# A float32 hybrid decoder block on one core: weights' high parts first and low parts after them in each projection, the first two projections interleaved, tokens in eight pieces, and TensorE kept on a constant before the first layer norm

## The chip, the core and the metric

The kernel runs on one core of one Trainium2 chip. The metric is the device time in microseconds (us) of one execution. Beside it stands one profiled execution, whose trace gives the start and length of each engine's instructions: TensorE (PE; its weight loads are PEld), VectorE (DVE), ScalarE (ACT), GpSimd (POOL) and SyncE (SP), which issues most transfers. Columns and ns are as the profile prints them.

## The reference, cut to what matters

One layer, 256 tokens of 2048 features, all in float32:

```python
h = layer_norm(x, emb_ln_g, emb_ln_b)
mix = hybrid_mixer(h, w_in, ...)          # see below
h = layer_norm(ALPHA * h + mix, ln1_g, ln1_b)
ffn = conv_ffn(h, w_ffn_up, ffn_conv_w, ffn_conv_b, w_ffn_down)
h = layer_norm(ALPHA * h + ffn, ln2_g, ln2_b)

def hybrid_mixer(x, w_in, ..., w_out):
    h = x @ w_in                          # 2048 -> a, gate, q, f, i, og, 1024 each
    u = causal_dwconv(a * sigmoid(gate), conv_w, conv_b)      # 31 taps
    u = silu(group_layer_norm(u))                             # 8 groups of 128
    fg = lb + (1 - lb) * sigmoid(f)       # lb: gate bounds, from a softmax over lb_logits
    o = hgrn2_recurrence(silu(q), 1 - fg, i, log(fg))         # 8 heads of 128
    o = rms_norm(o) * hgrn_norm_g * silu(og)
    return concatenate([u, o]) @ w_out

def conv_ffn(x, w_up, conv_w, conv_b, w_down):                # 2 x 5632 features
    g, v = split(x @ w_up)
    return (silu(causal_dwconv(g, conv_w, conv_b)) * v) @ w_down
```

## The kernel before

Every big product is made with float32r operands in three matmuls: an operand is split into a high part (its float32r rounding) and a low part (the rest), and high x high, high x low and low x high are added up in PSUM. Weights come in 196 chunks `raw` of 1 MB (two buffers); ACT copies each half of a chunk to `wh`, DVE subtracts to get `wl` (six buffers each). This is `stream`. The tokens, transposed to features x tokens, stand in `xT`: for each of 16 tiles `k` of 128 features 256 columns of high parts and 256 of low parts.

- A **feature unit** (`mm_features`, used for gate, a, f, q and the FFN's up projection) makes 2 x 128 output features for 256 tokens. For each k and each of its two accumulators it issues one matmul with `wh` over the 512 columns of `xT[k]` and one with `wl` over the 256 high columns: 32 pairs.
- A **token unit** (`mm_tokens`: v, og, the output projection, the down projection) uses tokens as the stationary operand, and issues three matmuls of 512 columns per k and token tile.

`UNITS` gives the mixer's order: ("ag", 0) is gate and a of the first 256 channels, then ("ag", 1), ("v", 0) and so on. Between the halves of a unit `pump()` lets generators advance: the 31 tap operations of a convolution on DVE (L368), its norm `conv_tail` (transposes L377 on PE, statistics L384 and L386 on DVE, the power on POOL L387/L388, L390 on DVE, ACT L392, transposes back L396 on PE), and the recurrences. Four PSUM banks hold accumulators (`acc`), four hold everything else (`ps`).

The start: four transfers of 512 KB bring the tokens `z`; DVE makes the statistics of the two token tiles (L284, L165), POOL the reciprocal root (L166, L167), ACT normalises tile 0 and DVE tile 1 (L179, L181); 32 transposes (L200) in eight groups of two k-tiles; ACT or DVE apply gain and bias (L187, L189), ACT writes the high part and DVE the low part of `xT` (L205). The second layer norm (ln1) lies between the last token units of the mixer and the first FFN unit; there tile 0 is normalised and transposed while PE still works on tile 1.

The tile framework orders each engine's instructions by priority in program order and by a cost model; `tc.issue_after` adds an order without a wait. Each engine executes its instructions in that order. It also gives transfers eight semaphores in turn, so that a ninth is issued only when the first has landed.

Of the kernel before, what the change touches and what calls it, by code (L numbers as in the profile page):

```python
# [34 lines left out]
PAD = 48  # L35
LEVELS = (1, 2, 4, 8, 16, 32, 64)
# [24 lines left out]
def hybrid_block(ctx, tc, x, wts, par, masks, ident_in, emb_g, emb_b, ln1_g, ln1_b, ln2_g, ln2_b, out):  # L61
# [15 lines left out]
    xv = x[0].rearrange("(t p) d -> p t d", p=P)  # L77
    for t in range(2):
# [3 lines left out]
    ident = const.tile([P, P], F32, name="ident")  # L82
    DMA.dma_start(out=ident, in_=ident_in)
# [7 lines left out]
    load_chunk()  # L91
    ps_par = const.tile([P, NPAR], F32, name="ps_par")
    DMA.dma_start(out=ps_par, in_=par)

# [10 lines left out]
    def stream(n):  # L105

        for _ in range(n):
            if nhalf[0] // 2 + 1 < wts.shape[0]:
                load_chunk()
            raw = raws.pop(0)  # L110
            for h in range(2):
# [3 lines left out]
                with ExitStack() as order:  # L115
                    order.enter_context(tc.high_priority(offset=AHEAD if nhalf[0] > 3 else 0))
                    for ins in behind.pop(nhalf[0], ()):
                        order.enter_context(tc.issue_after(ins.ins))
                    S.activation(wh, r, AF.Copy)  # L119
                    V.tensor_tensor(wl, r, wh.bitcast(F32), ALU.subtract)  # L120
# [41 lines left out]
    def layer_norm_stats(st):  # L162
# [3 lines left out]
        G.tensor_scalar(rs, mv[:, 1:2], LN_EPS, None, ALU.add)  # L166
        G.tensor_tensor(rs, rs, mhalf[:, 0:1], ALU.pow)  # L167
        return mv, rs

    def normalise(t, mv, rs, engines):  # L170

        if S in engines:
            nm = small.tile([P, 1], F32, name="nm")
            G.tensor_scalar(nm, mv[:, 0:1], -1.0, None, ALU.mult)
            G.tensor_tensor(nm, nm, rs, ALU.mult)
# [15 lines left out]
    def transpose_split(tiles, nk, gname, bname):  # L191
# [3 lines left out]
        for k0 in range(0, KT, nk):  # L195
# [10 lines left out]
            if tiles[-1] == 1 and (k0 + nk) % 4 == 0:  # L206
                behind[nhalf[0] + (k0 + nk) // 4] = made
# [14 lines left out]
    def mm_features(nch):  # L222


        acc = [accp.tile([P, 2 * T], F32, name="acc") for _ in range(2)]
        k = 0
        for wh, wl in stream(2):
            for kk in range(4):
                for j in range(2):
                    cs = slice(kk * 256 + j * P, kk * 256 + (j + 1) * P)  # L230
# [4 lines left out]
                k += 1  # L235
            pump()
        return acc
# [42 lines left out]
    stats = []  # L280
    for t in range(2):
# [3 lines left out]
        stats.append(layer_norm_stats(st))  # L285
    normalise(0, *stats[0], (S, S, S, S))
    normalise(1, *stats[1], (V, V, V, V))
# [17 lines left out]

    mk = const.tile([P, P + 64 * (len(LEVELS) - 1)], F32, name="mk")
    DMA.dma_start(out=mk, in_=masks)


    lb = const.tile([P, NT], F32, name="lb")  # L310
    omlb = const.tile([P, NT], F32, name="omlb")
    lmax = small.tile([P, NT], F32, name="lmax")
    le = small.tile([P, 2, NT], F32, name="le")
    lsum = small.tile([P, NT], F32, name="lsum")
    V.tensor_tensor(lmax, pc("lg0", 0, NT), pc("lg1", 0, NT), ALU.max)
    V.tensor_tensor(le[:, 0], pc("lg0", 0, NT), lmax, ALU.subtract)
    V.tensor_tensor(le[:, 1], pc("lg1", 0, NT), lmax, ALU.subtract)
# [190 lines left out]
    for kind, i in UNITS:  # L508
        run[kind](i)
# [204 lines left out]
```

## Time and profile before

| | |
|---|---|
| three runs | 1174.7, 1178.58 and 1179.71 us, median 1178.58 |
| the profiled execution | 1176.21 us, of which the span from first to last instruction is 1174.4 us |
| busy | PE 1141.5 us (97%), PEld 978.1, DVE 836.4 (71%), ACT 579.3 (49%), POOL 20.9 |
| chain that ended last | PE 92%, DVE 5% |
| granted TensorE clock | 0.995 over the span |
| transfers | 217.62 MB, mean 185 GB/s; a chunk `raw` of 1 MB lands 4.8 us after its issue (median) |

A busy share is a sum over stages, and PE's includes time that overlaps between matmuls, so what a stage costs is read from the starts of successive instructions. The views used are the waits per engine, the timeline (start, length, instruction, how often, and in brackets the idle time of the engine before it and what ended it), the groups of instructions in a stretch, and the windows (busy time of each engine in a stretch).

### The profile page before, as it was taken

What the parts mean: (1) busy time and instruction counts of PE and PEld (TensorE: products, weight loads), DVE (VectorE), ACT (ScalarE), POOL (GpSimd) and SP (SyncE); (2) the same over time, 40 slices, a digit from 0 to 9 for tenths busy, and PEclk for the clock granted to TensorE, in tenths of its full rate; (3) what the DMA queues carried; (4) which work ended last, traced back from release to release, by engine and by line L of the source; (5) the groups of instructions that cost most, each with busy time, mean ns of one, the idle gap of its engine ahead of it and who ended that gap; (6) DMA issues with size and microseconds to landing.
All of it is one profiled execution on the core that took longest, in us unless ns stands there. A gap on an engine that the chain in (4) does not pass through costs nothing.

```text
span 1174.4 us, 15650 instructions
## 1 busy us (share of the span) xinstructions
PE 1141.5 (97%) x6102; PEld 978.1 (83%) x6102; DVE 836.4 (71%) x1307; ACT 579.3 (49%) x826; POOL 20.9 (2%) x41
## 2 busy tenths in 40 slices
PE   5999999999999989999999999999999999999996
PEld 4887888888888868888888888888888888888885
DVE  7799999998697787666666668444566666665555
ACT  6545655646444355555555553333455554554330
POOL 1000000000000000000000000000000000000001
PEclk9999999999999999999999999999999999999998
DMA  5654544454455536655555557555555555555551
GB/s 217 231 200 179 184 175 148 176 179 144 148 175 188 198 117 246 213 186 184 196 195 180 189 206 233 198 197 184 199 190 181 179 188 193 193 179 183 208 182 72
DMA packets 33050, 217.62 MB, mean 185 GB/s; under 512 B 3664, under 2 KB 3792, under 8 KB 7632
## 3 DMA queue, kind: packets, MB, share of 16 engines
q1 hardware_dynamic: 32112, 214.53, 51.6%
q10 hardware_dynamic: 864, 2.10, 0.5%
q8 instruction: 48, 0.79, 0.3%
q14 instruction: 26, 0.21, 0.1%
HBM read 214.51 MB, written 2.10 MB: 184 GB/s over the span
## 4 chain that ended last, share of the span: by engine, by line
PE 92%; DVE 5%; issue 1%; POOL 1%; DMA 1%; ACT 0%; DVEq 0%; SPq 0%; ACTq 0%
PE acc L231 36%; PE acc L233 19%; PE acc L248 11%; PE acc L250 11%; PE acc L249 11%; PE ps L450 2%; DVE wl L120 1%; DVE y L368 1%; DMA z<-in_x 1%; DVE xT L205 0%; DVE full L189 0%; DVE z L584 0%; DVE z L581 0%; PE ps L200 0%; PE ps L439 0%
## 5 line engine op out<-in xcount | busy, mean ns | idle before, releaser
L231 PE MATMUL acc<-xT,wh 128*128 128x512 f32 x1920 | 674.9, 396 | 0.2
L120 DVE TENSOR_TENSOR wl<-raw,wh 128x1024 fp32r<-128x1024 f32 x392 | 477.8, 1222 | 238.2 <-ACT wh L119 237.8
L119 ACT ACTIVATE wh<-raw 128x1024 fp32r<-128x1024 f32 x392 | 412.1, 1057 | 379.4 <-PE acc L250 203.9
L233 PE MATMUL acc<-xT,wl 128*128 128x256 f32 x1920 | 539.1, 281 | 0.8 <-DVE wl L120 0.8
L231 PEld LDWEIGHTS acc<-xT,wh 128*128 128x128 f32 x1920 | 360.3, 188 | 83.6 <-DVE xT L205 0.7
L233 PEld LDWEIGHTS acc<-xT,wl 128*128 128x128 f32 x1920 | 363.1, 189 | 1.7 <-DVE wl L120 1.5
L249 PE MATMUL acc<-wl,acthi 128*128 128x512 f32 x350 | 136.2, 389 | 0.0
L250 PE MATMUL acc<-wh,actlo 128*128 128x512 f32 x350 | 136.2, 389 | 0.0
L248 PE MATMUL acc<-wh,acthi 128*128 128x512 f32 x350 | 136.2, 389 | 0.0
L368 DVE SCALAR_TENSOR_TENSOR y<-upad,ps_par,y 128x256 f32<-128x256 f32 x240 | 102.6, 476 | 0.0
L241 ACT ACTIVATE tb<-acc 128x256 f32<-128x256 f32 x120 | 44.7, 377 | 81.4 <-PE acc L233 81.4
L250 PEld LDWEIGHTS acc<-wh,actlo 128*128 128x128 f32 x350 | 65.7, 188 | 13.8
L249 PEld LDWEIGHTS acc<-wl,acthi 128*128 128x128 f32 x350 | 65.7, 188 | 13.7
L248 PEld LDWEIGHTS acc<-wh,acthi 128*128 128x128 f32 x350 | 65.7, 188 | 13.5
L248 PE MATMUL acc<-wh,xT 128*128 128x512 f32 x128 | 51.2, 400 | 0.0
L248 PE MATMUL acc<-wh,mixhi 128*128 128x512 f32 x128 | 51.1, 399 | 0.0
L250 PE MATMUL acc<-wh,mixlo 128*128 128x512 f32 x128 | 50.4, 393 | 0.0
L250 PE MATMUL acc<-wh,xT 128*128 128x512 f32 x128 | 50.2, 392 | 0.0
L249 PE MATMUL acc<-wl,mixhi 128*128 128x512 f32 x128 | 50.1, 392 | 0.0
L249 PE MATMUL acc<-wl,xT 128*128 128x512 f32 x128 | 49.9, 390 | 0.0
L567 ACT ACTIVATE acthi<-vv 128x256 fp32r<-128x256 f32 x44 | 18.4, 418 | 53.7 <-DVE vv L566 53.7
L242 DVE TENSOR_TENSOR gpad<-acc,tb 128x256 f32<-128x256 f32 x44 | 18.7, 424 | 25.2 <-ACT tb L241 25.2
(125 smaller groups left out, 711.3 us busy)
## 6 DMA issues: line engine op xcount, KB each, us to landing
raw<-in_wts SPq DMA_DIRECT2D x196, 1024.0 KB, 4.8
z<-in_x ACTq DMA_DIRECT2D x2, 512.0 KB, 5.9
z<-in_x SPq DMA_DIRECT2D x2, 512.0 KB, 5.7
gb<-in_emb_g SPq DMA_DIRECT2D x4, 256.0 KB, 3.4
bb<-in_emb_b SPq DMA_DIRECT2D x4, 256.0 KB, 4.5
gb<-in_ln_g SPq DMA_DIRECT2D x4, 256.0 KB, 4.4
bb<-in_ln_b SPq DMA_DIRECT2D x4, 256.0 KB, 4.7
g<-in_ln_g SPq DMA_DIRECT2D x1, 1024.0 KB, 4.7
```

What stands on the lines that cost most here:

```text
L119: S.activation(wh, r, AF.Copy)
L120: V.tensor_tensor(wl, r, wh.bitcast(F32), ALU.subtract)
L231: PE.matmul(acc[j], lhsT=wh[:, cs], rhs=xT[:, k, :], start=k == 0, stop=False, skip_group_check=True)
L233: PE.matmul(acc[j][:, T:], lhsT=wl[:, cs], rhs=xT[:, k, 0:T], start=False, stop=k == KT - 1, skip_group_check=True)
L241: S.activation(tb, acc[:, T:], AF.Copy)
L242: V.tensor_tensor(dst, acc[:, 0:T], tb, ALU.add)
L248: PE.matmul(acc, lhsT=hi(k + i), rhs=wh[:, cs], start=k + i == 0, stop=False)
L249: PE.matmul(acc, lhsT=hi(k + i), rhs=wl[:, cs], start=False, stop=False)
L250: PE.matmul(acc, lhsT=lo(k + i), rhs=wh[:, cs], start=False, stop=k + i == nk - 1)
L368: V.scalar_tensor_tensor(y[i], ups[i][:, k:k + T], pc("conv_w", c * TAPS + k), y[i], ALU.mult, ALU.add)
L450: PE.matmul(sp[0:m, 2 * i + s], lhsT=K[:, i, s * P:s * P + m], rhs=rhs, start=True, stop=True)
L567: S.activation(acthi[:, slot], vv, AF.Copy)
```

## The change

- **Feature units run in two passes** (`high`, `low`): all 32 matmuls with `wh`, then all 32 with `wl`. `pump` stays at four calls per unit.
- **The first unit ("ag", 0) interleaves gate and a** (`mm_features_by_k(2)`): for each half chunk the gate's high and low matmuls, then those of a; the weights are laid out so that chunks come in that order. Four accumulators are in use.
- **The first FFN unit goes by token tile** (`mm_features_by_tile`): the high matmuls of tile 0 over all k (2 x 128 columns each), then those of tile 1 with the low ones.
- Tokens load in eight pieces of 256 KB, alternating between the SP and ACT queues; the identity after the first four, parameters before the first `raw`.
- 28 matmuls over a zeroed part of `xT` are issued to PE ahead of everything (`WARM`).
- The gate bounds (`masks_and_bounds`, seven small DVE operations, one on ACT, one transfer) follow the first unit.
- In ln1, tile 0 is normalised on ACT, tile 1 in turns on DVE and ACT; the product of minus the mean is one DVE operation (`minus_mean`).

```diff
+WARM = 28
...
-        for c in range(2):
-            eng = DMA if c == 0 else S
-            eng.dma_start(out=z[:, t, c * 1024:(c + 1) * 1024], in_=xv[:, t, c * 1024:(c + 1) * 1024])
...
+        for c in range(4):
+            eng = (DMA, S)[c % 2]
+            eng.dma_start(out=z[:, t, c * 512:(c + 1) * 512], in_=xv[:, t, c * 512:(c + 1) * 512])
+        if t == 0:
+            DMA.dma_start(out=ident, in_=ident_in)
...
+    idle = xT[:, KT - 1, :]
+    V.memset(idle.bitcast(F32), 0.0)
+    blank = psp.tile([P, 512], F32, name="ps")
+    for n in range(WARM):
+        PE.matmul(blank, lhsT=idle[:, 0:P], rhs=idle, start=True, stop=True)
...
-            if tiles[-1] == 1 and (k0 + nk) % 4 == 0:
-                behind[nhalf[0] + (k0 + nk) // 4] = made
+            mark[0] = made
+            n = (k0 + nk) // 4
+            if (k0 + nk) % 4 == 0 and len(tiles) == 2:
+                behind[nhalf[0] + 2 * n, "high"] = behind[nhalf[0] + 2 * n + 1, "high"] = made
...
-    def mm_features(nch):
...
-                    PE.matmul(acc[j], lhsT=wh[:, cs], rhs=xT[:, k, :], start=k == 0, stop=False,
-                              skip_group_check=True)
-                    PE.matmul(acc[j][:, T:], lhsT=wl[:, cs], rhs=xT[:, k, 0:T], start=False,
-                              stop=k == KT - 1, skip_group_check=True)
...
+    def high(acc, wh, n):
+
+        for kk in range(4):
+            for j in range(2):
+                PE.matmul(acc[j], lhsT=wh[:, kk * 256 + j * P:kk * 256 + (j + 1) * P], rhs=xT[:, 4 * n + kk, :],
+                          start=n + kk == 0, stop=False, skip_group_check=True)
+
+    def low(acc, wl, n):
+
+        for kk in range(4):
+            for j in range(2):
+                PE.matmul(acc[j][:, T:], lhsT=wl[:, kk * 256 + j * P:kk * 256 + (j + 1) * P],
+                          rhs=xT[:, 4 * n + kk, 0:T], start=False, stop=4 * n + kk == KT - 1,
+                          skip_group_check=True)
...
+        acc, lows = new_acc(), []
+        for n, (wh, wl) in enumerate(stream(2)):
+            high(acc, wh, n)
+            lows.append(wl)
+            if n in (1, 2):
+                pump()
+        for n, wl in enumerate(lows):
+            low(acc, wl, n)
+            if n in (0, 3):
+                pump()
+        return acc
+
+    def mm_features_by_k(count):
+
+
+        accs = [new_acc() for _ in range(count)]
+        for n, (wh, wl) in enumerate(stream(2 * count)):
+            high(accs[n % count], wh, n // count)
+            low(accs[n % count], wl, n // count)
+        return accs
+
+    def mm_features_by_tile():
...
+        for t in range(2):
+            for n, (wh, wl) in enumerate(parts):
+                for kk in range(4):
+                    for j in range(2):
+                        PE.matmul(tile_of(acc[j], t), lhsT=wh[:, kk * 256 + j * P:kk * 256 + (j + 1) * P],
+                                  rhs=tile_of(xT[:, 4 * n + kk, :], t), start=t + n + kk == 0, stop=False,
+                                  skip_group_check=True)
+                if t == 1:
+                    low(acc, wl, n)
         return acc
...
-        acc = mm_features(2)
+        acc, acc_a = mm_features_by_k(2) if p == 0 else (mm_features(), None)
...
-        acc = mm_features(2)
+        acc = acc_a or mm_features()
...
-                        normalise(t, *layer_norm_stats(st1[t]), (V, V, V, V))
+                        mv, rs = layer_norm_stats(st1[t])
+                        normalise(t, mv, rs, minus_mean(mv, rs, V)[0], (V, S, V, S) if t else (S, S, S, S))
...
-        acc = mm_features(2)
+        acc = mm_features() if j else mm_features_by_tile()
```

How the instructions stand on PE at the start of the program (`ps` are transposes, `acc` matmuls of the first unit; widths are the columns streamed), before:

```order
L200 MATMUL ps<-ident,z 128x128 x24
L231 MATMUL acc<-xT,wh 128x512 x2
L200 MATMUL ps<-ident,z 128x128 x8
L233 MATMUL acc<-xT,wl 128x256 x2
L231 MATMUL acc<-xT,wh 128x512
L233 MATMUL acc<-xT,wl 128x256
```

and of the changed program (L172 is the constant, L219 the transposes, L251 `high`, L258 `low`):

```order
L172 MATMUL ps<-xT 128x512 x28
L219 MATMUL ps<-ident,z 128x128 x24
L251 MATMUL acc<-xT,wh 128x512 x5
L219 MATMUL ps<-ident,z 128x128 x4
L251 MATMUL acc<-xT,wh 128x512 x3
L258 MATMUL acc<-xT,wl 128x256 x4
L219 MATMUL ps<-ident,z 128x128 x4
L258 MATMUL acc<-xT,wl 128x256 x4
```

The constant stands ahead of all transposes; eight high matmuls and then eight low ones replace the pairs, and the last two groups of transposes lie inside the first eight of each.

The second convolution's norm on DVE (`cst` and `cmv` are its statistics, `cnm` minus the mean times the root that POOL makes of `cmv`, `wl` the low part of a later weight, `y` taps of the next convolution), before:

```order
L384 BN_STATS cst<-ps 128x6 x4
L386 BN_AGGR cmv<-cst 128x2 x4
L120 TENSOR_TENSOR wl<-raw,wh 128x1024
L390 SCALAR_TENSOR_TENSOR cnm<-cmv,crs 128x4
L368 SCALAR_TENSOR_TENSOR y_1440<-upad_215,ps_par,y_1440 128x256
```

and of the changed program:

```order
L436 BN_STATS cst<-ps 128x6 x4
L438 BN_AGGR cmv<-cst 128x2 x3
L125 TENSOR_TENSOR wl<-raw,wh 128x1024
L438 BN_AGGR cmv<-cst 128x2
L420 SCALAR_TENSOR_TENSOR y_1522<-upad_251,ps_par,y_1522 128x256
L442 SCALAR_TENSOR_TENSOR cnm<-cmv,crs 128x4
```

A `wl` now stands ahead of the fourth aggregate, for which POOL waits, and a tap ahead of `cnm`.

PE behind the last token matmul of the mixer, where ln1's second token tile is transposed (`ps<-ident,z`) and the first FFN unit begins, before:

```order
L250 MATMUL acc<-wh,mixlo 128x512
L200 MATMUL ps<-ident,z 128x128 x10
L231 MATMUL acc<-xT,wh 128x512
L233 MATMUL acc<-xT,wl 128x256
L231 MATMUL acc<-xT,wh 128x512
L200 MATMUL ps<-ident,z 128x128 x2
```

and of the changed program (L301 are the high matmuls by token tile):

```order
L319 MATMUL acc<-wh,mixlo 128x512
L301 MATMUL acc<-xT,wh 128x2x128 x24
L219 MATMUL ps<-ident,z 128x128 x12
L301 MATMUL acc<-xT,wh 128x2x128 x13
L219 MATMUL ps<-ident,z 128x128 x2
L301 MATMUL acc<-xT,wh 128x2x128 x3
```

24 matmuls that need only token tile 0 now stand ahead of the transposes of tile 1; the other eight of tile 0 stand behind twelve of them.

## Rows read from the trace of the kernel before

**Rows 1.** Waits of PE, whole run: us in total, times, longest us.

```profile
PE ps L200 <- ACT z L179: 11.1, 1, 11.1
PE ps L200 <- DVE z L181: 5.6, 3, 4.0
PE ps L396 <- ACT tmp L392: 3.4, 2, 2.8
PE acc L233 <- DVE wl L120: 0.8, 2, 0.5
```

**Rows 2.** Timeline of PE: pairs, then a token unit, then the last 256-column matmuls.

```profile
619.62 0.39 PE L231 MATMUL acc<-xT,wh 128*128 128x512 f32 x1
...
622.74 0.39 PE L231 MATMUL acc<-xT,wh 128*128 128x512 f32 x1
...
699.82 0.39 PE L250 MATMUL acc<-wh,actlo 128*128 128x512 f32 x1
...
703.90 0.39 PE L250 MATMUL acc<-wh,actlo 128*128 128x512 f32 x1
...
1162.15 0.28 PE L613 MATMUL ps<-wh,acthi 128*128 128x256 f32 x1
...
1163.47 0.28 PE L615 MATMUL ps<-wh,actlo 128*128 128x256 f32 x1
```

**Rows 3.** Timeline of the start, engines mixed; the last row begins pair 65.

```profile
5.41 3.21 DVE L284 BATCH_NORM_STATS2 st<-z 128x6 f32<-128x512 f32 x5 [5.41 <-DMA z<-in_x]
8.54 0.25 DVE L165 BATCH_NORM_AGGREGATE mv<-st 128x2 f32<-128x24 f32 x1
...
10.23 2.93 ACT L179 ACTIVATE z<-z,nm,rs 128x512 f32<-128x512 f32 x4 [2.77 <-POOL nm L175]
...
11.83 1.92 DVE L181 TENSOR_SCALAR z<-z,mv,rs 128x512 f32<-128x512 f32 x4 [1.01 <-POOL rs L167]
...
16.89 0.50 PE L231 MATMUL acc<-xT,wh 128*128 128x512 f32 x1
...
42.27 0.39 PE L231 MATMUL acc<-xT,wh 128*128 128x512 f32 x1
```

**Rows 4.** The page's transfers: issues, KB each, median us from issue to landing.

```profile
out<-z SPq DMA_DIRECT2D x4, 256.0 KB, 2.4
```

**Rows 5.** Groups of ACT and DVE between 11 and 31 us: busy us, mean ns.

```profile
L119 ACT ACTIVATE wh<-raw 128x1024 fp32r<-128x1024 f32 x6 | 6.2, 1051 | 0.0
...
L120 DVE TENSOR_TENSOR wl<-raw,wh 128x1024 fp32r<-128x1024 f32 x6 | 7.1, 1217 | 0.0
L205 DVE TENSOR_TENSOR xT<-full,xT 128x512 fp32r<-128x512 f32 x8 | 5.2, 684 | 1.2 <-ACT xT L205 1.2
L189 DVE TENSOR_SCALAR full<-ps,ps_par 128x256 f32<-128x256 f32 x8 | 4.1, 538 | 0.2
```

**Rows 6.** Timeline of PE: transposes of the start, early and late.

```profile
12.70 2.98 PE L200 MATMUL ps<-ident,z 128*128 128x128 f32 x13
...
16.11 0.71 PE L200 MATMUL ps<-ident,z 128*128 128x128 f32 x5
```

**Rows 7.** Window behind ln1: us, PE busy, granted clock, DMA share, GB/s.

```profile
428.89:432.29 3.40, 3.40 (x12) 0.50 0.33 137
```

**Rows 8.** Timeline of the first convolution's norm: transposes, statistics, transposes back.

```profile
106.03 0.60 PE L377 MATMUL ps<-ident,y 128*128 128x128 f32 x4
...
109.39 0.87 DVE L384 BATCH_NORM_STATS2 cst<-ps 128x6 f32<-128x128 f32 x4
...
112.87 0.33 PE L396 MATMUL ps<-ident,tmp 128*128 128x128 f32 x1 [2.84 <-ACT tmp L392]
```

**Rows 9.** Timeline of PE at ln1: transposes of tile 1; second FFN unit's first matmul.

```profile
427.56 0.86 PE L200 MATMUL ps<-ident,z 128*128 128x128 f32 x6 [4.00 <-DVE z L181]
...
442.82 0.39 PE L231 MATMUL acc<-xT,wh 128*128 128x512 f32 x1
```

**Rows 10.** Window in the mixer: us, busy PE, PEld, DVE, ACT, POOL, clock, DMA, GB/s.

```profile
100.00:200.00 100.00, 97.07 (x561) 83.95 (x560) 94.90 (x201) 58.33 (x89) 4.75 (x5) 1.00 0.50 179
```

More of the change, by code (lines that the diff above doesn't have):

```diff
@@ L116, in stream @@
                     order.enter_context(tc.high_priority(offset=AHEAD if nhalf[0] > 3 else 0))
-                    for ins in behind.pop(nhalf[0], ()):
+                    for ins in behind.pop((nhalf[0], "high"), ()):
                         order.enter_context(tc.issue_after(ins.ins))
                     S.activation(wh, r, AF.Copy)
+                    for ins in behind.pop((nhalf[0], "low"), ()):
+                        order.enter_context(tc.issue_after(ins.ins))
                     V.tensor_tensor(wl, r, wh.bitcast(F32), ALU.subtract)
@@ L165, in layer_norm_stats, with minus_mean, normalise @@
         V.bn_aggr(mv, st)
-        G.tensor_scalar(rs, mv[:, 1:2], LN_EPS, None, ALU.add)
-        G.tensor_tensor(rs, rs, mhalf[:, 0:1], ALU.pow)
-        return mv, rs
[L170 to L175, printed above, removed]
+        with ExitStack() as order:
+            if after is not None:
+                order.enter_context(tc.issue_after(after.ins))
+            G.tensor_scalar(rs, mv[:, 1:2], LN_EPS, None, ALU.add)
+            G.tensor_tensor(rs, rs, mhalf[:, 0:1], ALU.pow)
+        return mv, rs
+    def minus_mean(mv, rs, engine):
+        nm = small.tile([P, 1], F32, name="nm")
+        if engine is V:
+            return nm, V.scalar_tensor_tensor(nm, mv[:, 0:1], -1.0, rs, ALU.mult, ALU.mult)
+        G.tensor_scalar(nm, mv[:, 0:1], -1.0, None, ALU.mult)
+        return nm, G.tensor_tensor(nm, nm, rs, ALU.mult)
+    def normalise(t, mv, rs, nm, engines):
         for c, engine in enumerate(engines):
@@ new lines, in low, with new_acc, mm_features @@
+    def low(acc, wl, n):
[4 more added lines that the diff above has]
+                          skip_group_check=True)
+    def new_acc():
+        return [accp.tile([P, 2 * T], F32, name="acc") for _ in range(2)]
+    def mm_features():
+        acc, lows = new_acc(), []
[9 more added lines that the diff above has]
+        return acc
@@ L277, in mm_tokens @@
                     finish(n, t, accs[n, t])
-    stats = []
+    last = None
     for t in range(2):
@@ L284, in hybrid_block @@
             V.bn_stats(st[:, c], z[:, t, c * 512:(c + 1) * 512])
[L285 to L287 removed]
+        mv, rs = layer_norm_stats(st, last)
+        if t == 0:
+            nm, last = minus_mean(mv, rs, G)
+        normalise(t, mv, rs, nm, (V, V, V, V) if t else (S, S, S, S))
     transpose_split((0, 1), 2, "emb_g", "emb_b")
@@ L659, in _layout @@
         else:
-            for name in (("gate", "a") if kind == "ag" else ("f", "q")):
-                parts.append(_chunks(w_in, COL[name] + 256 * i, 256, 0, KT))
+            pair = [_chunks(w_in, COL[name] + 256 * i, 256, 0, KT)
+                    for name in (("gate", "a") if kind == "ag" else ("f", "q"))]
+            if (kind, i) == UNITS[0]:
+                halves = [c.reshape(2, P, 2, 1024).transpose(0, 2, 1, 3) for c in pair]
+                pair = [np.stack(halves, axis=2).transpose(0, 1, 3, 2, 4).reshape(4, P, 2048)]
+            parts.extend(pair)
     for k0, k1 in PASSES:
```

65 lines of the change are left out of this document (34 added, 31 removed).

## The prediction

> **What bounds the kernel now.** I read the page first (PE busy 97%, and on 92% of the chain that ended last), then what PE waits for, then the starts of its matmuls. The waits over the whole run come to some 21 us [rows 1]: 11.1 before the first transpose, 5.6 for normalised tokens (4.0 of it in one piece at ln1), 3.4 for the norm of a convolution, and only 0.8 for `wl`. All else is PE's own pace, and that is even [rows 2]: nine pairs in 3.12 us, 0.3467 us a pair; 18 matmuls of 512 columns one after the other in 4.08 us, 0.2267 each; eleven of 256 columns in 1.32 us, 0.1200 each. So a change of 2% is the most that all waits together hold, and the pace decides what more there is.
>
> **Two passes per feature unit.** A pass of 512s and a pass of 256s cost 0.2267 + 0.1200 = 0.3467 us for what was a pair: exactly the pair. The 256s of the last token unit follow each other with other weights each time, as the low pass does, so its weight loads are in that number. Over 1920 pairs I put nothing. Starts are printed to 0.01 us, which over 9, 18 and 11 intervals leaves some 1 ns a pair: 2 us to either side, kept for the range. That `wl` is needed later brings PE at most the 0.8 us that it waited for it.
>
> **The start.** Before, the tokens' statistics begin at 5.41, when the first 512 KB piece has landed, five of them last until the aggregate at 8.54, ACT normalises from 10.23, DVE from 11.83, and the first pair starts at 16.89 [rows 3]. A 256 KB piece by itself landed in 2.4 us [rows 4]; issued at some 0.7 that is 3.1 at the earliest, and 5.4 (no gain) at the latest. I take 4.0, since half the bytes of what was in flight by 5.41 are ahead of it. Five statistics then end at 7.1, and the chain behind them is unchanged: ACT from 8.8, DVE from 10.4, 1.4 us earlier each. On SP's queue the eight smaller pieces have a price: the ninth transfer waits for the first to land, so the parameters are issued at 4.0 and the first `raw` at some 5.4, when the third piece has landed. With 4.8 us to land, and more where the tokens still move, it is there by 11; ACT wants it at 12.7 (below).
>
> From there by engine, with the lengths of [rows 3, 5]. DVE: four pieces of tile 1 until 12.3, two `full` until 13.2. ACT: four pieces of tile 0 until 11.7, two `full` until 12.7, the first `wh` 13.7. DVE: the first `wl` 14.9, the low part of the first group of `xT` 15.5. So PE's first high matmul starts at 15.5, 1.4 before the old one.
>
> Then comes the larger gain. Until pair 65 PE took 42.27 - 16.89 = 25.4 us for 64 pairs that need 22.2, plus eight transposes [rows 3, 6]. It waited because four k-tiles gave it 8 pairs, 2.8 us, while DVE needed one `wl`, two low parts and two `full`, 1.2 + 2 x 0.68 + 2 x 0.54 = 3.7 us [rows 5]. With gate and a interleaved four k-tiles give 16 pairs, 5.5 us, against DVE's 4.9 (one more `wl`). PE becomes the slower one and goes through: 15.5 + 22.2 + 0.9 for transposes + some 0.3 = 38.9. Behind it the next unit needs accumulators that DVE empties after its fourth `wl` of that unit; I allow 0.1. **-3.3 us**, between -2.3 (first piece no earlier, PE through) and -4.
>
> The 28 constant matmuls stand ahead of the transposes. Early transposes stand (2.98 - 0.42) / 12 = 0.213 us apart, those from 16.11 on 0.11 [rows 6]: half rate and full rate. If the constant starts at some 1.3 and a third of it runs at half rate (2 x 0.227 a matmul), it takes 9 x 0.45 + 19 x 0.227 = 8.4 us and ends at 9.7, before the first transposes at about 11: nothing on the path. What it saves is transposes that were at half rate, and of these only the first group (4 x 0.10) is waited for; that is below what I can tell. Here a rule of the Trainium skill would say otherwise: "TensorE: Matmul & The Clock Gate", Part 4, has it that transposes do not count as activity for the clock gate. By that page nothing from 9.7 to 15.5 would hold the clock, and the first matmuls would run at half rate. The rows show the transposes' own spacing halve in an unbroken run of transposes, so here they do count, and I follow the rows.
>
> **The middle.** In the first convolution's norm the transposes back start 3.48 us behind the first statistics, and these were late because DVE had a backlog (109.39 against transposes issued at 106.03) [rows 8]; PE waited 2.8. In the changed order only 12 high matmuls (2.7 us) stand between the two groups of transposes, not 3.6 us of pairs. But DVE's work up to the statistics is the same (82 taps for 78, 25 `wl` for 26), while PE arrives as much earlier as the start gains less one microsecond, which the table load and the sigmoid cost, now behind all four `tb` copies. I expect DVE to be 0.5 to 1.5 late instead of 2.8: a wait of about 2, -0.8. In the second norm a `wl` (1.2 us [rows 5]) now stands ahead of the fourth aggregate: +1.2, since POOL and all behind it wait. In the third 13 matmuls of 0.227 (2.9 us) cover a chain that had 4.0 us of cover; the norms behind the first cost 3.4 - 2.8 = 0.6 together before [rows 1]: +0.7, as the rest of the missing cover lies beside a recurrence's small matmuls. One recurrence has its transposes back 4.0 us of PE work behind its product where 5.2 stood before: +0.4. **+1.5 us**, from -2 (no DVE lateness at all) to +4.
>
> **ln1.** Tile 0: ACT's four pieces in a row (0.7 each) replace DVE's four, which an addition and a statistic interrupt; PE's transposes wait a little more, and its token matmuls end 0.2 later, at about 423.6. Before, PE then sat idle for 4.0 us until 427.56 and ran 3.4 us at a granted clock of 0.50, 1.2 GHz [rows 7, 9]; the unit ended at 442.82. Now 24 matmuls x 0.12 = 2.9 us that need only tile 0 fill the idle stretch. But DVE sets the end: its aggregate comes at 426.5 (one low part more ahead of it), two pieces of tile 1 end at 428.7, and then it has four `wl` (1.15 apart, a little under [rows 5]), eight `full` and eight low parts of half the width of [rows 5] (0.33 and 0.35, somewhat over half of the time there), and one low part of the full width: together 10.6: 439.3. PE needs 4 x 0.12 + 8 x 0.12 = 1.4 more: 440.8. The two 256s for one 512 cost 0.4, inside it. **-2.0 us**, from -3.5 to 0.5, the latter if transposes behind the four `ps` buffers hold PE.
>
> **At no cost:** the bounds' seven small DVE operations (0.16 to 0.2 each) move behind the last low part, where PE has some 8 us of work queued; without that cover they cost 1.2.
>
> **The sum**: -3.3 + 1.5 - 2.0 = -3.8, so 1176.2 - 3.8 = 1172.4 against the profiled execution. The median of the runs is 2.4 above it, the mean of all four 1177.3; I go from the mean: 1173.5.
>
> **Rivals.**
> *The start's gain is lost in the middle.* The tile framework has reordered DVE, ACT and PE everywhere, and three of four norms of convolutions have less cover. For it: DVE is busy 94.9 of 100 us there [rows 10], so lateness does not heal. Each norm with 1 us more: +4, which leaves 1176.
> *Waits vanish.* With `wl` needed a pass later, DVE's lateness costs nothing, the first norm's 2.8 goes, ln1 gives 3.5: -3.3 - 2 - 3.5 = -8.8, 1168.5. Against it: the chain POOL to ACT is 3.48 us whatever DVE does.
> *The clock falls before the first matmuls.* PE has some 4 us without matmuls and some 2 without anything between 9.7 and 15.5; after 4.0 us of idleness at ln1 the granted clock was 0.50 for 3.4 us, which costs 1.7 us of work [rows 7, 9]. Then the sum is -2.1: 1175.2. The page named above would bring this about; the spacing in [rows 6] speaks against it.
> *The constant never runs at full rate*: 28 x 0.45 = 12.7 us ends at 14, the transposes come 3 us late, the start's gain is gone: 1176.8.
> *Slower: `wl` buffers hold up DVE.* A unit keeps four of six until its low pass, 32 x 0.227 = 7.3 us after its start. DVE is in order: if its next `wl` waits, taps behind it wait. DVE has 5.1 us of slack per 100 [rows 10], 14 us over the mixer. There are 14 two-pass products; held 1.7 us in each, DVE is 24 us behind, 10 beyond its slack, and the kernel is slower by over 0.5%, at 1184 or more. Against it: the two free buffers are a pass ahead.
>
> **How the numbers follow.** The forecast 0.45; start lost in the middle 0.2; waits vanish 0.14; clock falls 0.1; constant at half rate 0.04; buffers 0.07. One execution and the next differ by up to 0.4% here (1174.7 to 1179.7), so 0.5%, 5.9 us, is about what can be told from no change. From 1178.58, faster means below 1172.7: all of the vanishing waits and about two fifths of the forecast, by its range and the runs' spread, 0.34; slower 0.08; within 0.5% 0.58. The range holds all but the buffers: low end 1168 (waits vanish), high end 1180 (start lost and a high run). The forecast by itself holds 1170 to 1177.
>
> **What the profile after would show.** The first high matmul near 15.5 and the 65th near 39; the transposes 0.11 apart from the first; a low pass at 0.120 a matmul; ACT and DVE done with `xT` some 8 us before PE is done with the first unit; waits of 1 to 2 us in each norm of a convolution; the first FFN unit 2 us shorter. A low pass at over 0.122, a first `wl` later than 15, or DVE waiting on PE in the mixer would make it wrong.

## The result, and the profile after

The changed kernel takes 1170.3 us (median of five runs, 1169.85 to 1170.99). The kernel before, run beside it, took 1179.71 (median of five, 1174.7 to 1183.29). The ratio is 0.9922, 95% interval 0.9897 to 0.9948. Of the 88 runs of the kernel before that stand beside the kernels of this study 57 are below 1177.5 and 31 above 1178, median 1176.6, so those five lay high: the gain over the middle of all 88 is 6.3 us, and between the two profiled executions 5.7 (spans 1174.4 and 1168.7). The forecast was 1173.5, a gain of 3.8.

By stretches of PE, from the start of the first matmul of each to that of the next (us), the forecast's terms beside them:

| stretch | before | after | difference | forecast |
|---|---|---|---|---|
| start and first unit, to the first token unit | 64.45 | 63.87 | -0.58 | -3.3 |
| rest of the mixer, to its last token matmul | 358.72 | 358.11 | -0.61 | +1.5 |
| ln1 and first 24 FFN units | 274.80 | 274.18 | -0.62 | -2.0 |
| first down projection | 130.60 | 130.58 | 0 | 0 |
| last 20 FFN units | 226.12 | 222.24 | -3.88 | 0 |
| second down projection and tail | 119.73 | 119.72 | 0 | 0 |

Two thirds of the gain lie in a stretch for which the prediction had put nothing. In the timeline of PE after, the last 20 FFN units begin and end so:

```profile
826.74 7.42 PE L251 MATMUL acc<-xT,wh 128*128 128x512 f32 x32
834.00 4.00 PE L258 MATMUL acc<-xT,wl 128*128 128x256 f32 x32
837.83 2.46 PE L251 MATMUL acc<-xT,wh 128*128 128x512 f32 x10
...
1048.98 0.40 PE L317 MATMUL acc<-wh,acthi 128*128 128x512 f32 x1
```

640 pairs' work takes 222.24 us, 0.3473 a pair; a high pass 7.26, a low pass 3.83, 0.227 and 0.120 a matmul. In the trace of before the same stretch, which [rows 2] do not touch, reads:

```profile
828.57 0.39 PE L231 MATMUL acc<-xT,wh 128*128 128x512 f32 x1
...
900.28 0.40 PE L231 MATMUL acc<-xT,wh 128*128 128x512 f32 x1
...
902.40 0.40 PE L231 MATMUL acc<-xT,wh 128*128 128x512 f32 x1
...
1054.69 0.40 PE L248 MATMUL acc<-wh,acthi 128*128 128x512 f32 x1
```

Six pairs in 2.12 us are 0.3533 each, and all 640 took 226.12: 0.3533. So pairs have a second pace, 6.7 ns above that of [rows 2]. Neither busy time nor waits tell of it: in the windows view (behind the length the busy times of PE, PEld, DVE, ACT and POOL, then the granted clock, DMA share and GB/s) PE is busy for all of it, with a granted clock of 1.00, before and after:

```profile
830.00:1050.00 220.00, 220.00 (x1248) 190.86 (x1247) 140.99 (x192) 114.07 (x173) 0.00 (x0) 1.00 0.53 187
```

```profile
830.00:1046.00 216.00, 216.00 (x1243) 191.16 (x1242) 135.22 (x190) 116.01 (x173) 0.00 (x0) 1.00 0.51 190
```

Over the whole trace of before, pairs are 5.5 us above 0.3467 each: 4.25 here, 1.2 in the mixer, nothing in the 23 units of [rows 2].

**The waits after**, beside [rows 1]:

```profile
PE ps L448 <- ACT tmp L444: 2.7, 4, 1.1
PE ps L219 <- ACT z L198: 2.4, 2, 1.5
PE ps L219 <- DVE z L200: 1.8, 2, 1.3
...
PE ps L551 <- DVE tmp L547: 1.2, 2, 0.7
PE acc L251 <- ACT wh L122: 0.9, 1, 0.9
```

**The start after**, beside [rows 3, 6] (timeline, engines mixed):

```profile
1.44 8.42 PE L172 MATMUL ps<-xT 128*128 128x512 f32 x28 [1.44 <-DVE xT L169]
5.00 2.63 DVE L353 BATCH_NORM_STATS2 st<-z 128x6 f32<-128x512 f32 x4 [3.61 <-DMA z<-in_x]
8.21 0.69 DVE L353 BATCH_NORM_STATS2 st<-z 128x6 f32<-128x512 f32 x1 [0.58 <-DMA z<-in_x]
8.82 0.24 DVE L177 BATCH_NORM_AGGREGATE mv<-st 128x2 f32<-128x24 f32 x1
10.50 2.93 ACT L198 ACTIVATE z<-z,nm,rs 128x512 f32<-128x512 f32 x4 [3.45 <-POOL nm L191]
12.38 1.91 DVE L200 TENSOR_SCALAR z<-z,mv,rs 128x512 f32<-128x512 f32 x4 [1.00 <-POOL rs L182]
12.98 5.17 PE L219 MATMUL ps<-ident,z 128*128 128x128 f32 x23 [1.29 <-DVE z L200]
17.80 1.92 PE L251 MATMUL acc<-xT,wh 128*128 128x512 f32 x5
41.64 0.63 PE L251 MATMUL acc<-xT,wh 128*128 128x512 f32 x2
63.87 0.40 PE L317 MATMUL acc<-wh,xT 128*128 128x512 f32 x1
```

The first high matmul comes at 17.80, 0.9 later than before, not 1.4 earlier. Before the first aggregate DVE stands idle for 0.58 us, for a fifth statistic that waits for its piece of the tokens. And the clock is not what the forecast assumed (windows of the same execution):

```profile
5.10:9.70 4.60, 4.60 (x21) 3.61 (x19) 3.88 (x7) 1.28 (x1) 0.47 (x3) 1.00 1.07 367
11.36:12.98 1.62, 0.33 (x1) 0.14 (x2) 0.61 (x3) 1.62 (x3) 0.80 (x2) 0.72 0.99 410
12.98:17.80 4.82, 4.82 (x23) 4.76 (x23) 4.19 (x8) 4.33 (x7) 0.00 (x0) 0.50 0.75 299
```

It is 1.00 in the second half of the constant (which ends at 9.86) and 0.50 for all 23 transposes. The 0.72 of the stretch before them says that it fell at some 12.1, when PE had run a single transpose since the constant.

**ln1 after**, beside [rows 7, 9] (timeline of PE, then windows):

```profile
422.20 2.07 PE L301 MATMUL acc<-xT,wh 128*128 128x256 f32 x16
424.76 1.19 PE L301 MATMUL acc<-xT,wh 128*128 128x256 f32 x8 [0.48 <-DVE xT L224]
426.47 1.09 PE L219 MATMUL ps<-ident,z 128*128 128x128 f32 x8 [0.53 <-DVE z L200]
...
437.90 0.86 PE L251 MATMUL acc<-xT,wh 128*128 128x512 f32 x3
...
440.02 3.13 PE L251 MATMUL acc<-xT,wh 128*128 128x512 f32 x13
444.07 2.11 PE L251 MATMUL acc<-xT,wh 128*128 128x512 f32 x8 [0.92 <-ACT wh L122]
```

```profile
424.00:440.00 16.00, 13.43 (x102) 12.12 (x101) 14.41 (x30) 11.18 (x23) 0.81 (x2) 1.00 0.56 202
```

The one idle stretch of 4.00 us is gone (PE is busy for 13.43 of these 16 us, its waits are 0.26 to 0.69 each), the clock stays at 1.00, and a new wait of 0.92 stands behind the unit.

### The profile page after: what moved, and what is told of

Read it like the earlier page. It is cut to its first block, busy times and chain, and to the rows that moved or that the text cites. A ratio compares the mean times of both kernels' runs of the same rounds, so it can differ in the third digit from the quotient of the medians.

```text
span 1168.7 us, 15745 instructions
## 1 busy us (share of the span) xinstructions
PE 1145.6 (98%) x6162; PEld 988.8 (85%) x6162; DVE 827.2 (71%) x1304; ACT 585.9 (50%) x832; POOL 20.9 (2%) x41
## 4 chain that ended last, share of the span: by engine, by line
PE 92%; DVE 4%; POOL 1%; ACT 1%; DMA 1%; issue 1%; DVEq 0%; ACTq 0%
PE acc L251 36%; PE acc L258 19%; PE acc L317 11%; PE acc L319 11%; PE acc L318 11%; PE ps L502 2%; DVE wl L125 1%; DMA z<-in_x 1%; PE ps L219 1%; DVE z L659 0%; DVE z L656 0%; POOL crs L440 0%; PE ps L491 0%; POOL oss L542 0%; DVE cst L436 0%
## 5 line engine op out<-in xcount | busy, mean ns | idle before, releaser
L125 DVE TENSOR_TENSOR wl<-raw,wh 128x1024 fp32r<-128x1024 f32 x392 | 465.4, 1221 | 180.5 <-ACT wh L122 112.3
L122 ACT ACTIVATE wh<-raw 128x1024 fp32r<-128x1024 f32 x392 | 406.4, 1055 | 316.4 <-PE acc L319 181.2
L251 PE MATMUL acc<-xT,wh 128*128 128x512 f32 x1888 | 446.1, 392 | 0.9 <-ACT wh L122 0.9
L251 PEld LDWEIGHTS acc<-xT,wh 128*128 128x128 f32 x1888 | 349.9, 188 | 70.8 <-ACT wh L122 1.3
L258 PEld LDWEIGHTS acc<-xT,wl 128*128 128x128 f32 x1920 | 239.3, 191 | 5.1
L258 PE MATMUL acc<-xT,wl 128*128 128x256 f32 x1920 | 241.6, 283 | 0.0
L319 PEld LDWEIGHTS acc<-wh,actlo 128*128 128x128 f32 x350 | 65.7, 188 | 13.4
L310 ACT ACTIVATE tb<-acc 128x256 f32<-128x256 f32 x120 | 39.5, 381 | 64.6 <-PE acc L258 64.6
L643 DVE TENSOR_TENSOR actlo<-vv,acthi 128x256 fp32r<-128x256 f32 x44 | 18.7, 425 | 67.2 <-ACT acthi L642 67.2
L636 ACT ACTIVATE y<-gpad,ps_par 128x256 f32<-128x256 f32 x44 | 26.5, 601 | 63.2 <-DVE gpad L311 63.2
```

What stands on the lines that cost most here:

```text
L251: PE.matmul(acc[j], lhsT=wh[:, kk * 256 + j * P:kk * 256 + (j + 1) * P], rhs=xT[:, 4 * n + kk, :], start=n + kk == 0, stop=False, skip_gro ...
L258: PE.matmul(acc[j][:, T:], lhsT=wl[:, kk * 256 + j * P:kk * 256 + (j + 1) * P], rhs=xT[:, 4 * n + kk, 0:T], start=False, stop=4 * n + kk = ...
L310: S.activation(tb, acc[:, T:], AF.Copy)
L319: PE.matmul(acc, lhsT=lo(k + i), rhs=wh[:, cs], start=False, stop=k + i == nk - 1)
L636: S.activation(y, g[:, 2:], AF.Identity, scale=pc("fcw", 3 * j + 2), bias=pc("fcb", j))
L643: mark[0] = V.tensor_tensor(actlo[:, slot], vv, acthi[:, slot].bitcast(F32), ALU.subtract)
```

## The experiments

Theory A: pairs of 512 and 256 columns have two paces, passes only one, and that is the gain. Rival B: the pace belongs to a place in the program, and start and ln1 made the gain.

**The kernel before, once more.** No edit. 

> The kernel before, once more, for a second profile. Theory A (two paces): a pair of 512 and 256 columns runs at 0.3467 us or at 0.3533 us, a whole stretch at a time, and which stretches are slow differs from execution to execution. In the profile of before 845 pairs were slow, 5.5 us; so this profile has another number of them, and its span is 1174.4 + 0.00665 x (that number - 845), within 0.7 us. Rival B (place): the slow pairs belong to their place in the program (what DVE and the transfers do there), so the same stretches, 828 to 1054 us above all, are slow again and the span is 1174.4 within 0.7.

1176.18 us (12 runs, ratio 0.9989, interval 0.9973 to 1.0005), span 1175.9. Pairs lie 6.7 us above 0.3467 each, where the first profile had 5.5: 1.2 more (some 180 pairs), and the span is 1.5 longer, within A's 0.7. The span alone proves little, since the first feature matmul also came 0.6 later (17.48 for 16.89). Its timeline, 30 pairs apart:

```profile
118.27 0.40 PE L231 MATMUL acc<-xT,wh 128*128 128x512 f32 x1
...
128.87 0.40 PE L231 MATMUL acc<-xT,wh 128*128 128x512 f32 x1
...
830.02 0.39 PE L231 MATMUL acc<-xT,wh 128*128 128x512 f32 x1
...
1056.14 0.40 PE L248 MATMUL acc<-wh,acthi 128*128 128x512 f32 x1
```

10.60 us for 30 pairs, 0.3533; in the first profile the same place reads

```profile
118.03 0.39 PE L231 MATMUL acc<-xT,wh 128*128 128x512 f32 x1
...
128.44 0.39 PE L231 MATMUL acc<-xT,wh 128*128 128x512 f32 x1
```

0.3467. So the same pairs of the same program run at either pace, as A says; but the last 20 units took 226.12 in both, as B says. A stretch kept its pace until something else came between its matmuls: in the first profile 725 pairs at 0.3467 and 640 at 0.3533 without a change. And pairs that follow straight on 512-column token matmuls, as at 828.57, were at 0.3533 in all four traces that have such pairs, wherever more than three of them stood together.

**Passes and nothing else.** In `mm_features` of the kernel before:

```diff
         for wh, wl in stream(2):
...
-                    PE.matmul(acc[j][:, T:], lhsT=wl[:, cs], rhs=xT[:, k, 0:T], start=False,
...
+            lows.append(wl)
...
+        for wl in lows:
...
+                    PE.matmul(acc[j][:, T:], lhsT=wl[:, cs], rhs=xT[:, k, 0:T], start=False,
```

> The kernel before with nothing but its feature units in two passes, the first unit and the first FFN unit too; start, normalisation, gate bounds and weights' layout as before. Theory A: no matmul of a pass is slower than 0.2267 or 0.120 us, the 5.5 us of slow pairs are gone and the runs lie within 1.5 us of each other: 1171 (1169 to 1173). Rival B: the pace stays what it was at its place, the gain came from start and ln1, and this runs like the kernel before: 1177 to 1180.

1177.19 us (12 runs within 1.5 us; ratio 0.9991, 0.9976 to 1.0007): no gain. Yet the last 20 units took 222.24. What passes give there they lose where tokens are late: the first unit ended at 67.61 for 64.45, and ln1 with the first 24 FFN units took 277.3 for 274.8. PE's waits for the tokens' low parts, which the kernel before does not have:

```profile
PE acc L231 <- DVE xT L205: 3.1, 5, 1.2
```

A pass asks for all 16 tiles of `xT` within 7.3 us, where pairs took 11.1. Theory A stands for the pace, but not by itself for the gain: theory C, that passes pay only where the first two units have other work, took its place.

**Pairs in the changed kernel.** `mm_features` back to one high and one low in turn; the first unit and the first FFN unit as changed. 

> The changed kernel with its feature units in pairs again (all but the first unit, which stays in blocks of eight, and the first FFN unit, which stays by token tile). Theory A: stretches at 0.3533 us a pair come back in some executions, the runs spread over 4 us or more and their median is 1173 to 1180; where an execution has no slow stretch it is at about 1170. Rival B: as the changed kernel, 1169.5 to 1171.5, all runs close together.

1177.56 us (12 runs, 1176.98 to 1178.15; ratio 0.9998, 0.9982 to 1.0014). Here the first 24 FFN units ran at the slow pace too, the place of [rows 2]:

```profile
600.06 0.40 PE L274 MATMUL acc<-xT,wh 128*128 128x512 f32 x1
...
602.18 0.40 PE L274 MATMUL acc<-xT,wh 128*128 128x512 f32 x1
```

Six pairs in 2.12, 0.3533; pairs are 10.9 us above 0.3467 in all. Against the middle of the runs before, all the rest of the change, with pairs, is worth nothing that can be measured. But that comparison mixes paces. Against the first profile the first unit ends 1.1 earlier (63.31), and of the 277.5 us behind the mixer 260.0 are 736 pairs at 0.3533, which leaves 17.4 for ln1 and the first FFN unit where 19.7 stood: 2.2 less. The slow pace of those 736 pairs takes 4.9 back. In all, the span is 1.4 longer (1175.8) with 5.4 us more of slow pairs, so between executions of equal pace the rest is worth some 4 us. From here to the changed kernel the span falls by 7.1 where 10.9 us of slow pairs go: 0.6 of the difference is the start, where the clock was low for longer, and some 3 us are what passes cost elsewhere. The spread of 4 us that I expected did not come; runs so close together would fit the slow pace in all of them, but one was profiled.

**Without the constant.** `WARM` and the zeroing taken out. 

> The changed kernel without the 28 constant matmuls and the zeroing they need. In its trace the granted clock fell back to 0.50 before the transposes, so if the constant brings nothing the first high matmul starts at 17.0 to 17.9 as there (17.80) and the time is 1170.3 within 0.7. If the constant does bring something, the transposes and the first matmuls run longer at half rate, the first high matmul starts after 18.5 and the time is 1171 to 1172.

1170.32 us (7 runs, one of them at 1175.95; ratio 0.9933, 0.9909 to 0.9957). The first high matmul started at 18.02 and the first unit ended at 63.94: where the clock falls behind it, as in the profile of the changed kernel (17.80 and 63.87), the constant brings next to nothing. Where it did not fall (the run with four pieces, below) the first unit ended at 63.06; the medians, 1170.32 and 1170.17, do not show it.

**Gate and a one after the other**, with the weights laid out for it.

```diff
-        acc, acc_a = mm_features_by_k(2) if p == 0 else (mm_features(), None)
+        acc, acc_a = mm_features(), None
```

> The changed kernel with gate and a of the first unit one after the other, each in two passes. Theory C (passes remove the slow pace, but need work that is ready): in the kernel of before with passes alone, the first unit's 128 pairs ended 3.2 us later than with pairs, since 16 high matmuls a k-tile group run ahead of the transposed tokens. So here the first unit ends at 66.5 to 68 us instead of 63.87 and the time is 1173 to 1174.5. Rival D (the first unit's lateness is taken up later by waits that shrink): 1170 to 1171.

1173.55 us (10 runs; ratio 0.9968, 0.9951 to 0.9984), first unit ended at 67.64. Its timeline shows the rests between groups of high matmuls:

```profile
26.31 2.11 PE L251 MATMUL acc<-xT,wh 128*128 128x512 f32 x8 [1.14 <-DVE xT L224]
29.43 1.42 PE L251 MATMUL acc<-xT,wh 128*128 128x512 f32 x5 [1.00 <-ACT wh L122]
```

**The first FFN unit in plain passes.**

```diff
-        acc = mm_features() if j else mm_features_by_tile()
+        acc = mm_features()
```

> The changed kernel with its first FFN unit in two plain passes. Theory C: from the mixer's last token matmul to the second FFN unit 21.0 to 22 us instead of 17.69, less the 1.1 us that the changed kernel waits right behind it: 1173 to 1174.5. Rival D: the normalisation on two engines made the gain, not the order of the matmuls: 18 to 18.7 us there, 1170 to 1171.5.

1173.26 us (10 runs; ratio 0.9969, 0.9955 to 0.9984). From the mixer's last token matmul to the first down projection 277.8 us instead of 274.2, though the wait behind the first unit is gone. PE idles for 4.20 us again, and the clock falls behind it, for longer than in [rows 7]:

```profile
426.61:430.00 3.39, 3.03 (x12) 2.11 (x12) 3.15 (x7) 3.20 (x7) 0.00 (x0) 0.50 0.67 278
430.00:436.00 6.00, 6.00 (x18) 4.65 (x18) 5.40 (x12) 4.06 (x11) 0.00 (x0) 0.55 0.46 175
```

Both point to C, against D.

**Fours in the kernel before.** Two 512s, then two 256s; `wl` is needed when it was.

```diff
                 for j in range(2):
                     cs = slice(kk * 256 + j * P, kk * 256 + (j + 1) * P)
                     PE.matmul(acc[j], lhsT=wh[:, cs], rhs=xT[:, k, :], start=k == 0, stop=False,
                               skip_group_check=True)
+                for j in range(2):
+                    cs = slice(kk * 256 + j * P, kk * 256 + (j + 1) * P)
                     PE.matmul(acc[j][:, T:], lhsT=wl[:, cs], rhs=xT[:, k, 0:T], start=False,
```

> The kernel before with its feature matmuls in fours: two of 512 columns, then two of 256, instead of 512, 256, 512, 256. Waits and all else stay. If it is a single 256 between two 512s that has two paces, fours run at 0.693 us each throughout, both FFN stretches take the passes' time (255.2 and 222.2 us), and the time is 1170 to 1172 with all runs within 1.5 us. If any short matmul before a long one can be slow, the stretches at 0.700 us or more a four remain, and the runs are 1175 to 1181 as before.

1173.96 us (10 runs within 1.8 us; ratio 0.9967, 0.9949 to 0.9986). Four fours:

```profile
899.87 0.63 PE L231 MATMUL acc<-xT,wh 128*128 128x512 f32 x2
...
902.66 0.62 PE L231 MATMUL acc<-xT,wh 128*128 128x512 f32 x2
```

2.79 us, and 222.92 for the last 20 units, 0.697 a four or 0.3483 a pair's work: between the two paces, and steady through both FFN stretches. One loop split in two gives 2.7 us against the 1176.7 beside it. Neither outcome came as expected: 0.693 and 1170 to 1172 were too low, and no stretch ran at 0.700.

**The clock held.** 34 constants, and one more behind each of the first five groups of transposes:

```diff
+            if len(tiles) == 2 and k0 // nk < HOLD:
+                with tc.issue_after(turned.ins):
+                    constant(1)
```

> The changed kernel with 34 constant matmuls instead of 28, and one more behind each of the first five groups of four transposes, so that TensorE is never long without a matmul before the first unit. If the clock fell because nothing but transposes ran from 9.7 us on, it stays at 1.00 here, the transposes stand 0.11 us apart, the first high matmul starts at 16 to 16.7 instead of 17.80, and the time is 1168.8 to 1169.8. If the clock falls as well, the first high matmul starts at 18 to 19 and the time is 1170.3 to 1171.5.

1169.96 us (7 runs; ratio 0.9936, 0.9914 to 0.9958). The clock stayed:

```profile
13.00:17.00 4.00, 3.90 (x28) 3.32 (x28) 3.63 (x8) 4.00 (x8) 0.00 (x0) 1.00 0.79 315
```

But the first high matmul started at 17.60, only 0.2 earlier, since PE then waits for DVE's low part of the tokens; the first unit ended at 63.22, 0.65 earlier. The 16 to 16.7 expected did not come.

```profile
17.60 1.43 PE L259 MATMUL acc<-xT,wh 128*128 128x512 f32 x5 [0.60 <-DVE xT L232]
```

**Tile 0's aggregate before tile 1's statistics**, on top of that, and the identity behind the tokens:

```diff
+            with ExitStack() as order:
+                if t:
+                    order.enter_context(tc.issue_after(aggr[0].ins))
+                V.bn_stats(st[:, c], z[:, t, c * 512:(c + 1) * 512])
```

> The kernel of the run with constants between the transposes, in which the clock stayed at 1.00 and the first high matmul started at 17.60. Here DVE also makes tile 0's aggregate before any statistic of tile 1, and the identity is the ninth transfer instead of the last token piece. If the start hangs on the tokens' statistics (the aggregate stood behind a statistic that waited for tile 1's piece until 8.60), the first aggregate comes at 7.5 to 8, ACT normalises from 9.3 to 9.7 instead of 10.90, and the first high matmul starts at 16.2 to 17.0: 1168.6 to 1169.6. If it hangs on DVE's weights or the gain and bias in front of the first low part, the first high matmul stays at 17.4 to 17.7 and the time at 1170.0.

1169.84 us (4 runs; ratio 0.9935, 0.9911 to 0.9959).

```profile
7.49 0.27 DVE L183 BATCH_NORM_AGGREGATE mv<-st 128x2 f32<-128x24 f32 x1
...
17.02 1.45 PE L260 MATMUL acc<-xT,wh 128*128 128x512 f32 x5 [0.56 <-DVE xT L233]
```

The aggregate comes 1.7 us earlier than there (9.21), the first high matmul 0.6. The rest is tile 1, whose normalisation starts at 11.94 for 12.50. The first unit ended at 62.74, but ln1 and the first 24 FFN units took 275.0 for 274.2, so the profiled execution hardly shows it. The granted clock fell there, though the matmuls that need only tile 0 were in place; in the other seven traces with them it did not:

```profile
428.04:431.45 3.41, 3.41 (x16) 3.41 (x17) 2.87 (x6) 2.58 (x8) 0.00 (x0) 0.50 0.12 19
```

**Tokens in four pieces in the changed kernel.** 

> The changed kernel with the tokens in four transfers of 512 KB, the identity behind them, as before the change. If eight pieces bring what the prediction gave them, 1.4 us of the start, the first high matmul starts 1 to 1.5 us later than 17.80, and the time is 1171.2 to 1172. If the pieces bring nothing, since the aggregate of tile 0 came later with eight (8.82) than with four (8.54) and the last piece is a ninth transfer, it starts at 17.0 to 17.9, and the time is 1169.7 to 1170.4.

1170.17 us (4 runs; ratio 0.9938, 0.9914 to 0.9962), first aggregate at 9.02, first high matmul at 17.41, first unit ended at 63.06. The fair comparison is the run that held the clock, as the clock stayed up here too: with eight pieces that had 9.21, 17.60 and 63.22. So eight pieces bring nothing. In this trace the same 28 constants ran at half rate for longer, ended at 10.97 instead of 9.86, and left the clock at 1.00 through the transposes (timeline, then window):

```profile
1.44 9.53 PE L171 MATMUL ps<-xT 128*128 128x512 f32 x28 [1.44 <-DVE xT L168]
```

```profile
12.90:15.60 2.70, 2.67 (x22) 2.39 (x23) 2.30 (x6) 2.70 (x6) 0.00 (x0) 1.00 0.88 347
```

**Weights' low parts free in the first FFN unit.**

```diff
-            elif (k0 + nk) % 4 == 0:
-                behind[nhalf[0] + n, "low"] = made[1:]
```

> The changed kernel without the order that puts each low part of the first FFN unit's weights behind the low parts of the tokens that it stands beside. In the changed kernel PE waited 0.92 us at 444.07 behind that unit: wh for a chunk that landed at 442.78, since it was issued at 438.01, when a low part of weights had left its buffer. If that chain is right, the chunk is issued 1 us or more earlier, the wait behind the unit goes and the second stretch of FFN units takes 255.3 to 255.6 us instead of 256.49; what the first FFN unit loses, as tokens' low parts now come later, is 0 to 1 us: 1169.4 to 1170.4. If ACT's order makes the wait (wh stands behind the gate's silu), it stays, and the time is 1170.3 to 1171.3.

1169.73 us (5 runs; ratio 0.9931, 0.9904 to 0.9958). The wait for `wh` is gone, but PE waits 1.3 us for tokens' low parts instead of 0.7, and the whole stretch to the first down projection takes 274.0 for 274.2. The chain (a low part frees `raw`, its transfer takes 4.8 us, ACT copies it) is right; the 0.9 us are moved, not saved.

**Passes in the FFN alone**, from its second unit on, in the kernel before:

```diff
-        acc = mm_features(2)
+        acc = mm_passes() if j else mm_features(2)
```

> The kernel before with two passes in the FFN units from the second on and nothing else changed; start, mixer, norms and ln1 keep pairs. If the slow pace of pairs is the main term of the gain, the stretch from 829 to 1055 us takes 222.2 us instead of 226.1 and the one before it 255.2 to 255.5 in every execution: 1176.3 - 3.9 = 1172.4 (1171.5 to 1173.5), with all runs within 2 us, where those of before lie 7 us apart. The rest of the change (start, mixer, ln1) would then be worth the remaining 2 us. If the gain sits in start and ln1, the time is 1175.5 to 1177.

1172.91 us (12 runs, 1171.97 to 1174.18; ratio 0.9961, 0.9944 to 0.9977). The last 20 units took 222.24, the 23 units before the first down projection 256.35, for the 255.2 to 255.5 expected (a wait of 0.4 for `wh` in it). With nothing moved at start, in the mixer or at ln1, this gives 3.8 us against the 1176.68 of the kernel before beside it, six tenths of the 6.3.

## Why the prediction was right, and where it was not

**The time came out at the low edge of the forecast's own range, 1170 to 1177, and for other reasons than the forecast's.** The step that failed is "All else is PE's own pace, and that is even", and with it that two passes cost "exactly the pair" and "Over 1920 pairs I put nothing", with 2 us to either side. The nine pairs of [rows 2] were taken from the one long stretch of that trace that ran at 0.3467. 5.5 us of the profiled execution were the second pace, and passes do not have it: 222.24 us in the last 20 units in all ten traces of kernels that run them in passes, 226.12 in all three with pairs. The three terms that the forecast did have, -3.8 in all, gave -1.8, less than half, and a stretch that it had at nothing gave -3.9. That the whole gain did not come out at half of what was forecast is luck. The ratio beside the five runs is a gain of 0.8%, past the 0.5% within which I had put 0.58 of the chances; against the middle of all 88 runs it is 0.5%.

**The start**, forecast -3.3, gave -0.6, by three sizes. The tokens: first statistic at 5.00 for 4.0, since the first piece, with others in flight, landed after 4.2 us (2.4 for a piece of the output, [rows 4]); then the aggregate at 8.82 for 7.1, as a statistic of tile 1 stands ahead of it and waits for its piece; so ACT at 10.50 for 8.8 and DVE at 12.38 for 10.4. That the order of DVE decides the aggregate the run with tile 0's first shows (7.49). The ninth transfer was not the parameters but tile 1's last token piece: it was issued at 5.16, when the first had landed, and its statistic waited 0.17 for it. The first `wl` began at 15.92, past the 15 that the prediction had named as a sign of being wrong; that DVE's two `full` end at 13.2 is a slip in its sum (12.3 and 2 x 0.54 make 13.4), on no path. The clock: 0.50 for all the transposes, the rival "the clock falls", which I gave 0.1. It costs 0.65 of the first unit, by the run that held it, less than I feared, as DVE's low part ends last anyway. The interleaving: 64 pairs' work in 41.64 - 17.80 = 23.84 us for 25.4, -1.5 where -2.0 was forecast. Without it passes would lose 3.8.

I followed [rows 6], in which transposes alone saw their spacing halve, against the Trainium skill's page "TensorE: Matmul & The Clock Gate", Part 4, by which transposes do not count. In the changed kernel 23 transposes stayed at 0.50, as that page of the Trainium skill would have it; but the clock had fallen before they began. And in the run with pairs in the changed kernel it came back while PE had nothing but transposes, from 13.00 to the first high matmul at 17.71:

```profile
13.17:16.58 3.41, 3.41 (x18) 3.41 (x18) 2.90 (x6) 3.32 (x6) 0.00 (x0) 0.50 0.89 341
16.59:17.70 1.11, 0.81 (x7) 0.57 (x5) 1.11 (x3) 1.11 (x2) 0.00 (x0) 1.00 0.08 30
```

So here transposes alone did bring the clock up, as [rows 6] have it, and the measurement decides against Part 4 of that page of the Trainium skill. What failed is the step that the clock would stay up between a constant that ends at 9.7 and the transposes: of the six traces with these 28 constants only the one with four pieces kept it throughout. The same page of the Trainium skill (Part 1, "What's actually happening") has the moment at which the clock rises vary from run to run. The traces agree: the same 28 constants ran for 8.42 us in one and 9.53 in the other, and the transposes at 0.50 and 1.00. [rows 6] alone could not tell which.

**The middle**, forecast +1.5, gave -0.6. The first norm's wait fell by 1.7 (2.8 to 1.1), where I gave -0.8; the waits of the other norms and of the recurrences' transposes grew by 1.8 (1.0 to 2.8, [rows 1] with 0.4 more for L396, and L448 and L551 above), where I gave 2.3. So waits are even, not +1.5. The 1.2 us of slow pairs that went with the passes were not in my sum; passes' own small gaps (0.4 per 20 units) give some of it back.

**ln1** was right in its step: the idle 4.00 us and the fall of the clock are gone. At 440.02 three matmuls (0.68) of the next unit are already done, so from the mixer's last token matmul it is 17.4 us for 19.7, -2.3 where -2.0 was forecast. What was not seen is the wait behind it: `wl` comes late, holds `raw`, and PE waits 0.92 at 444.07; with what passes themselves cost over the next 23 units (0.4) and around the wait, 1.7 are given back.

**At no cost**: the gate bounds' seven operations caused no wait of PE between 22 and 108 us in the trace after. The rival of the `wl` buffers has its wait, in the waits of DVE over the whole run after:

```profile
DVE wl L125 <- PE acc L258: 66.8, 43, 5.9
```

Only 2.4 us of it, two waits, lie between 42 and 420 us, where DVE waiting on PE was to be a sign of being wrong and where DVE is busy for 327 of 378; the rest is some 1.5 us a unit in the FFN, where DVE has room, and no wait of PE for `wl` is listed.

**Open.** What makes a stretch of pairs take one pace or the other was not settled, only that it changes when something comes between, and that no trace of passes, and not the one of fours, shows two paces. That the runs of the kernel before above 1178 are those whose first 24 FFN units have the slow pace (736 x 6.7 ns = 4.9 us) fits the kernels with passes or fours there, whose runs lie within 2.2 us of each other but for the one at 1175.95; it was only argued, as none of those runs was profiled. The run at 1175.95 is a warning: with no pairs there to be slow it took 5.6 us more than the median of its kernel, so something else can cost as much.

## What to carry to other kernels

Read an engine's pace in every long stretch, as its span divided by its count, not in one sample of nine: PE was 100% busy at full clock in both paces. Group matmuls of one width, at least by twos; a long pass also changes when operands are wanted, so the first unit behind late data needs another order (a second product, or a tile that is ready). When a wait goes, look one transfer further: here the next unit got most of it back.

## What the runs showed of the hardware that was not expected

The two paces: 512 and 256 columns in turn at 0.3467 or 0.3533 us a pair, the latter in a pattern of three pairs (0.361, 0.349, 0.350) that held for all 640 pairs; two and two at 0.3483; 32 and 32 at 0.3473. The granted clock rose from 0.50 to 1.00 at 16.58 with only transposes on PE since 13.00. And the granted clock of the transposes behind one and the same constant was 0.50 in one trace, where it had ended 3.1 us before them, and 1.00 in another, where it had run 1.1 us longer at half rate and ended 1.9 us before them.
